# T4's split behind the second pair's evictions, the third pair's products reordered, and C22's transposes placed in mid-slice

## The chip, the core and the metric

One Trainium2 chip (trn2), one NeuronCore of it. The metric is the device time of one execution in microseconds (us), as the median of several runs. TensorE multiplies, VectorE and ScalarE read its accumulators, GpSimd works between buffers, and SyncE issues most of the transfers.

## What is computed

A decoder block on 1024 positions of width 1024: a short gated convolution and a forgetting attention side by side, merged by gates, and then a gated feed-forward with a causal convolution of three taps. The change lies in the last part, the feed-forward, cut here to what matters:

```
h2 = rmsnorm(x, norm2_g) * (1 + sc2) + sh2
u = h2 @ w_up                       # (1024, 2 * 2816)
u = causal_dwconv(u, conv_ffn_w)    # three taps over positions
gate, val = split(u, 2)
ff = (silu(gate) * val) @ w_down    # (1024, 1024)
x = x + g2 * ff
```

All is float32. The kernel makes each product from three: it splits both operands into a high part (H, rounded to the matmul's input type) and a low part (L, the rest), and sums H x H, H x L and L x H in an accumulator.

## The kernel before

**The up projection.** It runs over 22 slices f of 128 gate and 128 value columns, each with one accumulator g (gate) and one v (value) of 128 x 1024, two banks each; four such accumulators exist. The first three slices, u0, u1 and u2 (called pairs here, of gate and value weights), use plain products: `plain(n, half)` multiplies one half of the weights' rows (n // 2) of gate or value (n % 2) with a block of h2 for one half of the positions. A product is twelve matmuls of 512 columns. The blocks are B11 and B21 (first half of positions) and B12 and B22 (second half).

The other 19 slices use Strassen's scheme in Winograd's form, with seven products p1 to p7 in place of eight, from B11, B21, B22 and the combinations T1 to T4 of blocks. Block B12 and combination T4 share one buffer (L1553), so T4 may be written only when u2's products from B12 are done; it is read by each slice's last product, p4.

**The order around the first slice.** From L1459 on the order on TensorE, VectorE, ScalarE and GpSimd is the order of the program text; SyncE's is chosen by the scheduler. L1765 to L1787 make T1 to T3 with u0's evictions in between. L1790 to L1792 are u2's eight products. Then follow T4's four high parts (ScalarE, `split_h`, L1446) and low parts (VectorE, `split_l`, L1452). Behind them stand u1's evictions: `scale_g` and `scale_v` (ScalarE, L1676), `taps_g` and `taps_v` (VectorE, L1680, two each), `silu` (ScalarE, L1702), `ff` (VectorE, L1705) and its store. Between them stands `U[3].x_split()`, which splits the first Strassen slice's weights x (wh on ScalarE, L93, wl on VectorE, L94). Then come that slice's sums of weights on GpSimd (L1593, L1594, L1599) and their splits (L1559, L1560). In the loop from L1809, p1 reads x, `snap` copies p1's bank to s1 (ScalarE, L1633), p7 writes the other bank of the same accumulator, and `u2` adds s1 into U2 (VectorE, L1625).

The buffers tagged u, eight of 128 x 1024, hold x1 (the block's input blocks, from which T1 to T4 are made) and later the evicted gate and value.

**The down projection.** Again seven products, in the order `ORDER = (1, 5, 6, 3, 7, 2, 4)`, each over eleven steps c of twelve matmuls into four banks e. In each step the operands of the step after next are split (ScalarE L1918, VectorE L1919). The four banks of a finished product are added to the output tiles xo in the next product's steps, one bank at a time (`x_add`, VectorE, L1950). A tile that is complete is turned in the step behind: four 128 x 128 transposes on TensorE into the bank just added (`x_turn_out`, L1961), a copy to ot (ScalarE, L1967) and the store (SyncE). Product 3 completes one tile for each e. Product 2 completes two, (0, 0) and (1, 1), which is C22, and both are turned in the same bank, one behind the other, in four steps of the last product (p = 4). Banks e = 0 and 1, and banks e = 2 and 3, are the two halves of one accumulator there.

Of the kernel before, what the change touches and what calls it, by code (L numbers as in the profile page):

```python
# [33 lines left out]
def tile_hybrid_block(  # L34
# [110 lines left out]
    NK = ND // 2  # L145
# [308 lines left out]
    class Token:  # L454
# [5 lines left out]
        def copy(self):  # L460
            q = f32(self.keep[:, 0]) if self.keep else bp.tile([P, 512], F32, tag="qn", name="q", bufs=6)
            scalar.activation(q, self.src, AF.Copy)
            self.src, self.copied = q, True
# [57 lines left out]
    def tok_mm(j, acc, cuts, units, t0):  # L521

        outs = [acc[:, 512 * i : 512 * i + c1 - c0] for i, (c0, c1) in enumerate(cuts)]
        for dd in range(ND):
            for f in events.pop(t0 + dd, ()):
                f()
            w = units[dd // 2]
            for t in TERMS:
                for o, (c0, c1) in zip(outs, cuts):
                    mm(o, h_slice(t[0], dd, j), w[t[1]][:, dd % 2, c0:c1],  # L530
                       start=dd == 0 and t == TERMS[0], stop=dd == ND - 1 and t == TERMS[2])
        return outs
# [142 lines left out]
    for i in range(8):  # L675
        t = T1K + TSK * i
# [220 lines left out]
    for n, j in enumerate((4, 5, 6, 7, 0, 1, 2, 3)):  # L897
# [7 lines left out]
        t = Token(j, tok_mm(j, acc, FULL, qunits, t0)[0], q_d, qg)  # L905
# [293 lines left out]
    steps = [(h, ip) for h in range(NH) for ip in range(4)]  # L1199
# [91 lines left out]
    def acc4(nm):  # L1291
        return psD.tile([P, S], F32, tag="acc", name=nm, bufs=4)
# [419 lines left out]
    def blocks(kk):  # L1712
        return x1[kk][:, lo], x1[kk][:, hi], x1[kk + NK][:, lo], x1[kk + NK][:, hi]
# [14 lines left out]
    def t_op(kk, n, low):  # L1728

        b11, b12, b21, b22 = blocks(kk)  # L1730
        dst, src, shift = ((T3, b12, db[:, kk : kk + 1]), (T2, b22, None), (T1, b11, None), (T4, b21, None))[n]
        (split_l if low else split_h)(dst, kk, src, shift)
# [4 lines left out]
    u0, u1, u2 = U[:N0]  # L1737
# [49 lines left out]
            U[3].fetch(up)  # L1787
    u2.xs = wsp[4:6]
    u2.g, u2.v = (acc4(nm) for nm in ("upg", "upv"))
    for n in (0, 2, 1, 3):  # L1790
        for half in range(2):
            u2.plain(n, half)  # L1792
    for kk in range(NK):
        t_op(kk, 3, False)
        t_op(kk, 3, True)
    u1.scale_g()
    u1.scale_v()
    u1.taps_g()
    u1.silu()
    U[3].x_split()  # L1800
    u1.taps_v()
    u1.ff()
    u1.ff_out()
# [64 lines left out]
    def ff_load(f, half):  # L1868
        sync.dma_start(ff[f][:, half], ff_d[f][:, half])
# [68 lines left out]
    steps = [Step(p, c) for p in ORDER for c in range(NC)]  # L1938

    def banks_for():  # L1940
        ts = [acc4("dn") for _ in range(2)]
        return [t[:, sl] for t in ts for sl in (lo, hi)]

    def x_add(p, e, bank, b0=0, nb=4):

        ij = ADDS[p]
        bl = slice(b0 * P, (b0 + nb) * P)
        t = xo[e, *ij][:, bl]
        g = g2[:, e + 4 * ij[0] : e + 4 * ij[0] + 1]
        vector.scalar_tensor_tensor(out=t, in0=bank[:, bl], scalar=g, in1=t, op0=ALU.mult, op1=ALU.add)  # L1950
        turns.extend((e, ij, bank) for ij in STORE.get(p, ()))

    def x1_load(e, i, j):
        sync.dma_start(xo[e, i, j], x1_d[e + 4 * i][:, hsl[j]])

    def x_turn_out(e, ij, bank, b0=0, nb=4, copy=None):

        i, j = ij
        bl = slice(b0 * P, (b0 + nb) * P)
        for n in range(b0, b0 + nb):  # L1960
            tensor.transpose(bank[:, n * P : (n + 1) * P],  # L1961
                             xo[e, i, j][:, n * P : (n + 1) * P], ident)
        ot = gp2.tile([P, 512], F32, tag="ot", name="ot", bufs=3)
        if copy:
            copy(ot[:, bl], bank[:, bl])
        else:
            scalar.activation(ot[:, bl], bank[:, bl], AF.Copy)  # L1967
        d0, t0 = (e + 4 * i) * P, 512 * j + b0 * P
        sync.dma_start(out[0, t0 : t0 + nb * P, d0 : d0 + P].rearrange("(j p) d -> p j d", p=P),
                       ot[:, bl].rearrange("p (j d) -> p j d", j=nb))  # L1970
# [18 lines left out]
    adds, turns = [], []  # L1989
    NE = 3  # L1990
    for t, st in enumerate(steps[: len(steps) - NE + 1]):
        n = t // NC
        if st.c == 0 and t:
            if n == 1:
                sets.append(banks_for())
            done, old = steps[t - 1].p, sets[(n + 1) % 2]
            adds = [lambda p=done, e=e, b=old[e]: x_add(p, e, b) for e in range(4)]
        banks = sets[n % 2]
        if t == T0:
            upS.close()  # L2000
            gp2 = ctx.enter_context(tc.tile_pool(name="ff2", bufs=1, side="left", reuse_waits="tile"))
            skeep += [gp2.tile([P, 512], F32, name=f"s{c}") for c in range(NC)]
            xo = {(e, i, j): gp2.tile([P, 512], F32, name=f"xo{e}{i}{j}") for e in range(4) for i, j in ((0, 0), (1, 1), (0, 1))}
            xo |= {(e, 1, 0): xo[e, 0, 1] for e in range(4)}
        for _ in range(2 if t < 26 else 1):
            if ff_loads:
                ff_load(*ff_loads.pop(0))
        for k in range(4 if t == 0 else t + AHEAD, min(t + AHEAD + 1, len(steps))):
            steps[k].load()
        for k in range(3 if t == 0 else t + 3, min(t + 4, len(steps))):  # L2010
            steps[k].sums()
        if st.p in X1 and T0 <= st.c < T0 + 4:
            x1_load(st.c - T0, *X1[st.p])
        if t + 2 < len(steps):
            steps[t + 2].split()
        for w in ends.get(t, ()):
            w()
        while turns:
            x_turn_out(*turns.pop(0))
        if st.c > 0 and adds and (st.c % 2 == 0 or st.p == ORDER[-1]):  # L2020
            adds.pop(0)()
        if t < len(steps) - NE:
            st.mm(banks)
    last = steps[-NE:]

    def finish(e):
# [47 lines left out]
```

## Time and profile before

| | us |
|---|---|
| median of three runs | 1474.64 |
| lowest and highest | 1472.72, 1478.87 |
| the profiled execution | 1473.5 |
| its span, first to last instruction | 1471.5 |

The profile's page gives for each engine its busy time, the share of the span and the number of instructions. Views of the trace give the same for stretches of time, list instructions of an engine in order of time with the idle time in front of each and what ended it, and name the wait that ended last. Times in the trace count from the span's start.

### The profile page before, as it was taken

To read this page: it belongs to the slowest core of one execution; us is meant where nothing else is said; L and a number is where in the kernel's file an instruction comes from. 1 tells how busy PE (TensorE), PEld (TensorE's weight loads), DVE (VectorE), ACT (ScalarE), POOL (GpSimd) and SP (SyncE) were. 2 spreads that over 40 slices of the span, in tenths; PEclk is the share of its full clock that TensorE was granted. 3 is DMA by queue.
4 is the path that set the end of the run, shared out by engine and by line. 5 is a ranking of instruction groups with operands and counts; after the bars stand their busy time and mean duration, and the time that the engine had idled before them with its cause. 6 is when DMAs were issued, how large, how long until landed. Compare 5 with 4: busy or idle time off the path is not lost. (4 is left out here: it accounts for less than half of the span.)

```text
span 1471.5 us, 19375 instructions
## 1 busy us (share of the span) xinstructions
PE 1403.4 (95%) x6668; PEld 1155.1 (78%) x6668; DVE 1099.4 (75%) x1828; ACT 651.8 (44%) x1104; POOL 504.1 (34%) x532
## 2 busy tenths in 40 slices
PE   5889889999999999899999999999999999999997
PEld 4679668887888888778788877888888887888876
DVE  7965798888777776456846858777777776898764
ACT  6554453434455454555414534333333333444443
POOL 3646666665555553323221013333333331000000
PEclk9999999999999999999999999999999999999999
DMA  9539654437664557776962122222222213983722
GB/s 286 160 105 322 199 163 129 132 95 209 159 169 115 146 133 227 225 244 219 244 164 83 44 72 86 86 87 86 86 86 86 72 36 116 390 311 103 213 80 77
DMA packets 260759, 222.44 MB, mean 151 GB/s; under 512 B 43117, under 2 KB 213445, under 8 KB 260661
## 3 DMA queue, kind: packets, MB, share of 16 engines
q1 hardware_dynamic: 259389, 218.61, 49.6%
q0 software_dynamic: 1136, 2.56, 0.6%
q8 instruction: 52, 0.85, 0.2%
q14 instruction: 46, 0.38, 0.1%
q10 hardware_dynamic: 136, 0.04, 0.0%
HBM read 169.76 MB, written 51.41 MB: 150 GB/s over the span
## 5 line engine op out<-in xcount | busy, mean ns | idle before, releaser
L1925 PE MATMUL dn<-bL,aH 128*128 128x512 f32 x308 | 120.5, 391 | 0.6 <-DVE bL L1919 0.6
L1925 PE MATMUL dn<-bH,aH 128*128 128x512 f32 x308 | 120.8, 392 | 0.0
L1925 PE MATMUL dn<-bH,aL 128*128 128x512 f32 x308 | 120.0, 390 | 0.0
L1559 ACT ACTIVATE wh<-ws 128x512 fp32r<-128x512 f32 x95 | 55.5, 627 | 133.8 <-POOL ws L1593 131.0
L730 DVE TENSOR_TENSOR ol<-ws,oh 128x512 fp32r<-128x512 f32 x98 | 94.6, 974 | 14.1 <-ACT oh L729 11.6
L94 DVE TENSOR_TENSOR wl<-ws,wh 128x1024 fp32r<-128x1024 f32 (+1 forms) x51 | 70.0, 1373 | 40.6 <-ACT wh L93 40.1
L729 ACT ACTIVATE oh<-ws 128x512 fp32r<-128x512 f32 x98 | 61.2, 626 | 70.9 <-PE pacc L775 38.6
L1593 POOL TENSOR_TENSOR ws<-ws 128x512 f32<-128x512 f32 x19 | 24.7, 1300 | 187.7 <-DVE wl L94 187.7
L1162 ACT ACTIVATE L<-L,mn 128x256 f32<-128x256 f32 (+6 forms) x56 | 46.4, 829 | 60.7 <-DVE mn L1160 58.9
L1165 POOL TENSOR_SCALAR L<-L,rs 128x384 f32<-128x384 f32 (+7 forms) x62 | 48.3, 779 | 69.8 <-DVE rs L1164 68.6
L1925 PEld LDWEIGHTS dn<-bL,aH 128*128 128x128 f32 x308 | 57.8, 188 | 14.1 <-DVE bL L1919 2.7
L1185 ACT ACTIVATE th<-pt 128x512 fp32r<-128x512 f32 (+1 forms) x80 | 43.5, 551 | 55.3 <-PE pt L1179 53.7
L559 POOL TENSOR_TENSOR ws<-ws 128x512 f32<-128x512 f32 x42 | 55.1, 1312 | 36.5 <-DVE ol L730 17.1
L1925 PEld LDWEIGHTS dn<-bH,aH 128*128 128x128 f32 x308 | 57.8, 188 | 12.3 <-ACT bH L1918 0.4
L1925 PEld LDWEIGHTS dn<-bH,aL 128*128 128x128 f32 x308 | 57.8, 188 | 11.9
L93 ACT ACTIVATE wh<-ws 128x1024 fp32r<-128x1024 f32 (+1 forms) x58 | 60.8, 1052 | 12.3 <-DMA ws<-in_w_branch_a_dram 4.1
L1560 DVE TENSOR_TENSOR wl<-ws,wh 128x512 fp32r<-128x512 f32 x76 | 64.2, 864 | 2.3 <-ACT wh L1559 2.3
L1918 ACT ACTIVATE aH<-dws 128x512 fp32r<-128x512 f32 x52 | 32.8, 631 | 74.6 <-issue 41.0
L1680 DVE SCALAR_TENSOR_TENSOR u<-upv,cwT,u 128x1023 f32<-128x1023 f32 (+1 forms) x44 | 56.4, 1282 | 10.7 <-ACT u L1676 9.9
L1186 DVE TENSOR_TENSOR tl<-pt,th 128x512 fp32r<-128x512 f32 (+1 forms) x80 | 50.3, 634 | 18.5 <-ACT th L1185 17.1
L439 POOL TENSOR_TENSOR wacc<-wacc,wa 128x256 f32<-128x256 f32 x48 | 43.5, 907 | 55.8 <-ACT wa L438 52.4
L1919 DVE TENSOR_TENSOR aL<-dws,aH 128x512 fp32r<-128x512 f32 x52 | 35.9, 690 | 34.2 <-ACT aH L1918 34.2
(561 smaller groups left out, 4503.0 us busy)
## 6 DMA issues: line engine op xcount, KB each, us to landing
wa<-in_w_ada_dram SPq DMA_DIRECT2D x48, 512.0 KB
dws<-in_w_down_dram SPq DMA_DIRECT2D x96, 256.0 KB
ws<-in_w_up_dram SPq DMA_DIRECT2D x44, 512.0 KB
ws<-in_w_in_dram SPq DMA_DIRECT2D x36, 512.0 KB
ff<-ff_d SPq DMA_DIRECT2D x44, 256.0 KB
ff_d<-u SPq DMA_DIRECT2D x21, 512.0 KB
xt<-in_x_dram SPq DMA_DIRECT2D x8, 512.0 KB
v_d<-vt SPq DMA_DIRECT2D x8, 512.0 KB
```

Of the source, the lines that this page charges most:

```text
L93: scalar.activation(wh[:, : n * m], ws[:, : n * m], AF.Copy)
L94: eng.tensor_tensor(out=wl[:, : n * m], in0=ws[:, : n * m], in1=f32(wh[:, : n * m]), op=ALU.subtract)
L559: gpsimd.tensor_tensor(out=o, in0=a, in1=b, op=ALU.subtract)
L729: scalar.activation(h, src, AF.Copy)
L730: eng.tensor_tensor(out=l, in0=src, in1=f32(h), op=ALU.subtract)
L1162: scalar.activation(L[:, :n], L[:, :n], AF.Exp, scale=-1.0, bias=mn, accum_out=sm)
L1165: eng.tensor_scalar(out=L[:, :n], in0=L[:, :n], scalar1=rs, scalar2=0.0, op0=ALU.mult, op1=ALU.add)
L1186: vector.tensor_tensor(out=flat[2][:, c0:], in0=flat[0][:, c0:], in1=f32(flat[1][:, c0:]), op=ALU.subtract)
L1559: scalar.activation(ops[0][:, sl], src, AF.Copy)
L1560: eng.tensor_tensor(out=ops[1][:, sl], in0=src, in1=f32(ops[0][:, sl]), op=ALU.subtract)
L1680: vector.scalar_tensor_tensor(out=u[:, s:], in0=acc[:, : S - s], scalar=cwT[:, 2 - s, n : n + 1], in1=u[:, s:], op0=ALU.mult, op1=ALU.add)
L1925: mm(banks[e], self.A[i][:, es_], self.B[j], start=self.p in FIRST and self.c == 0 and t == 0, stop=self.c == NC - 1 and t == 2, skip_grou ...
```

## The change

It has two places. In the up projection u2's eight products come in another order, with the two from B12 first; and T4's splits move from ahead of u1's `scale_g` to behind `U[3].x_split()`. In the down projection the first tile turned in a step stays ahead of the step's products; a second one is turned after the products of the first two banks, and the step's `x_add` now stands between the two.

```diff
@@ -1787,17 +1787,16 @@
     u2.g, u2.v = (acc4(nm) for nm in ("upg", "upv"))
-    for n in (0, 2, 1, 3):
-        for half in range(2):
-            u2.plain(n, half)
-    for kk in range(NK):
-        t_op(kk, 3, False)
-        t_op(kk, 3, True)
+    for n, half in ((0, 1), (1, 1), (0, 0), (2, 0), (2, 1), (1, 0), (3, 0), (3, 1)):
+        u2.plain(n, half)
     u1.scale_g()
     u1.scale_v()
     u1.taps_g()
     u1.silu()
     U[3].x_split()
+    for kk in range(NK):
+        t_op(kk, 3, False)
+        t_op(kk, 3, True)
     u1.taps_v()
     u1.ff()
     u1.ff_out()
@@ -2015,12 +2014,18 @@
-        while turns:
-            x_turn_out(*turns.pop(0))
+        first, second = turns[:1], turns[1:]
+        turns.clear()
+        for a in first:
+            x_turn_out(*a)
         if st.c > 0 and adds and (st.c % 2 == 0 or st.p == ORDER[-1]):
             adds.pop(0)()
-        if t < len(steps) - NE:
-            st.mm(banks)
+        st_es = (range(2), range(2, 4)) if second else (range(4),)
+        for n, es in enumerate(st_es):
+            if n:
+                x_turn_out(*second[0])
+            if t < len(steps) - NE:
+                st.mm(banks, es)
```

## Rows read from the trace of the kernel before

**Rows 1.** The page: engine, busy us (share of the span) xinstructions.

```profile
PE 1403.4 (95%) x6668; PEld 1155.1 (78%) x6668; DVE 1099.4 (75%) x1828; ACT 651.8 (44%) x1104; POOL 504.1 (34%) x532
```

**Rows 2.** Stretches: length, busy (x) PE, PEld, DVE, ACT, POOL, clock, DMA share, GB/s.

```profile
856.94:859.74 2.80, 2.80 (x14) 2.27 (x12) 0.00 (x0) 0.00 (x0) 0.00 (x0) 1.00 0.00 0
867.90:893.13 25.23, 21.33 (x86) 15.43 (x85) 20.64 (x21) 9.98 (x14) 10.34 (x8) 1.00 0.33 105
893.13:912.54 19.41, 19.41 (x85) 15.79 (x84) 15.40 (x17) 8.18 (x12) 7.34 (x6) 1.00 0.26 82
912.54:931.88 19.34, 19.34 (x85) 15.79 (x84) 15.06 (x17) 7.28 (x10) 6.45 (x6) 1.00 0.26 81
```

**Rows 3.** Timeline of TensorE, first slice: start, length, instruction, [idle before, releaser].

```profile
869.16 0.50 PE L1569 MATMUL upv<-B11H,wh 128*128 128x512 f32 x1 [0.87 <-ACT wh L93]
...
870.42 0.50 PE L1569 MATMUL upv<-B11H,wl 128*128 128x512 f32 x1 [0.53 <-DVE wl L94]
...
877.37 0.50 PE L1569 MATMUL upv<-T3H,wh 128*128 128x512 f32 x1 [1.34 <-ACT s L1633]
...
884.23 0.50 PE L1569 MATMUL upv<-T1H,wl 128*128 128x512 f32 x1 [0.56 <-DVE wl L1560]
...
887.39 0.47 PE L1569 MATMUL upg<-B22H,wh 128*128 128x512 f32 x1 [0.59 <-DVE U L1625]
```

**Rows 4.** Timeline of ScalarE ahead of the first slice.

```profile
860.64 2.73 ACT L1446 ACTIVATE T4H<-x 128x512 fp32r<-128x512 f32 x4 [19.14 <-PE upv L1569]
863.27 1.10 ACT L1676 ACTIVATE u<-upg,cwT 128x1024 f32<-128x1024 f32 x1
...
867.11 1.06 ACT L1702 ACTIVATE u<-u 128x1024 f32<-128x1024 f32 x1 [1.73 <-DVE u L1680]
868.07 1.04 ACT L93 ACTIVATE wh<-ws 128x1024 fp32r<-128x1024 f32 x1
```

**Rows 5.** Timeline of VectorE ahead of the first slice.

```profile
843.13 2.59 DVE L1680 SCALAR_TENSOR_TENSOR u<-upv,cwT,u 128x1023 f32<-128x1023 f32 x2
845.65 1.22 DVE L94 TENSOR_TENSOR wl<-ws,wh 128x1024 fp32r<-128x1024 f32 x1
...
861.30 2.79 DVE L1452 TENSOR_TENSOR T4L<-x,T4H 128x512 fp32r<-128x512 f32 x4 [11.44 <-ACT T4H L1446]
...
869.14 1.23 DVE L94 TENSOR_TENSOR wl<-ws,wh 128x1024 fp32r<-128x1024 f32 x1 [2.13 <-ACT wh L93]
870.28 2.60 DVE L1680 SCALAR_TENSOR_TENSOR u<-upv,cwT,u 128x1023 f32<-128x1023 f32 x2
```

**Rows 6.** Timeline of GpSimd, its first work in this part.

```profile
870.45 1.30 POOL L1593 TENSOR_TENSOR ws<-ws 128x512 f32<-128x512 f32 x1 [72.38 <-DVE wl L94]
```

**Rows 7.** Stretches of the down projection: one turn, two turns four times, none.

```profile
1371.33:1374.56 3.23, 3.23 (x18) 2.73 (x17) 3.23 (x6) 1.64 (x3) 0.00 (x0) 1.00 0.70 225
1430.58:1450.26 19.68, 15.38 (x81) 12.34 (x81) 10.25 (x16) 8.96 (x17) 0.00 (x0) 1.00 0.38 107
1450.26:1452.98 2.72, 2.72 (x13) 2.25 (x12) 1.90 (x3) 1.15 (x3) 0.00 (x0) 1.00 0.00 1
```

**Rows 8.** Timeline of TensorE, transposes of the steps with two turns.

```profile
1430.58 0.64 PE L1961 MATMUL dn<-ident,xo 128*128 128x128 f32 x4
1432.29 0.66 PE L1961 MATMUL dn<-ident,xo 128*128 128x128 f32 x4 [1.08 <-ACT ot L1967]
...
...
1447.03 0.66 PE L1961 MATMUL dn<-ident,xo 128*128 128x128 f32 x4 [1.05 <-ACT ot L1967]
```

**Rows 9.** Timeline of ScalarE, first copy of the first of these steps.

```profile
1431.65 0.58 ACT L1967 ACTIVATE ot<-dn 128x512 f32<-128x512 f32 x1
```

**Rows 10.** Timeline of VectorE in two of these steps.

```profile
1431.87 0.68 DVE L1919 TENSOR_TENSOR bL<-ff,bH 128x512 fp32r<-128x512 f32 x1
1433.61 0.75 DVE L1950 SCALAR_TENSOR_TENSOR xo<-dn,mod,xo 128x512 f32<-128x512 f32 x1 [1.06 <-ACT ot L1967]
...
1437.43 0.74 DVE L1950 SCALAR_TENSOR_TENSOR xo<-dn,mod,xo 128x512 f32<-128x512 f32 x1
```

## The prediction

> **What bounds the kernel now.** I read the page first: TensorE is busy 95% of the span, and no other engine over 75% [rows 1]. So a microsecond is won only where TensorE stands still, and only if nothing else is late at the same place. I then looked for its idle time after 780 us by a table of stretches and by its own timeline. In the loop over 19 feed-forward slices a slice takes 19.3 to 19.4 us with TensorE busy throughout, but the first one, counted from the last product of the third pair (u2), takes 25.23 [rows 2]. Five waits stand in it [rows 3]: two for the split of its weights x (wh, then wl), one for the copy s1 (snap), one for wl of the next weights, one for the U2 sum. The second place is the last phase (p = 4): the four steps that turn output tiles take 19.68 us together, against 2.72 for a step without turns and 3.23 for a step of an earlier phase with one turn [rows 7]. In each of the four the second turn's transposes wait about 1.1 us for ScalarE's copy of the first (1.08 in the first step, 1.05 in the fourth) [rows 8]. The granted clock is 1.00 in all these stretches [rows 2, 7], so no term for the clock enters.
>
> **Why the first slice is late.** ScalarE stands idle for 19.14 us, until 860.64, because its next four instructions write T4 over B12 and wait for u2's products from B12; VectorE idles 11.44 us behind it [rows 4, 5]. Queued behind on the same two engines are u1's evictions (scale, taps, silu) and the split of the first slice's weights, whose wh ends at 869.11 and wl at 870.37 [rows 4, 5]. TensorE had finished u2 at 868.13 (last start 867.90 plus 0.23). GpSimd's sums for the same slice wait for that wl, after 72.38 us of idleness [rows 6].
>
> **Part 1, order of u2's products.** The eight products are the same, 2.80 us each [rows 2]; nothing is added. They start at 845.74 (four of them before 856.94). Those from B12 become first and second, so B12 is free at 845.74 + 5.60 = 851.3 instead of 862.5. The price is cover: the first product into u2.v moves from 856.94 to 848.54. Its accumulators are those of u0.v, whose last tap ends at 845.72, and its weights are split by 846.87 [rows 5]. That leaves 2.8 and 1.7 us; below that each microsecond would be lost once. I cost it at nothing. u2.g is complete one product later, 859.74, far ahead of its eviction.
>
> **Part 2, T4 behind u1's evictions.** ScalarE is free at 841.50 (860.64 less 19.14) and VectorE at 849.86 (861.30 less 11.44) [rows 4, 5]. With durations of these rows, and buffers u taken as free only when VectorE's last T split ends: scale_g 849.9 to 851.0, taps_g (2.60) to 853.6, silu (1.06) to 854.7, x wh (1.04) to 855.7, x wl (1.23) to 857.0. Then T4's high parts on ScalarE to 858.4 (2.73; B12 is free since 851.3) and low parts on VectorE to 859.8 (2.79), taps_v to 862.4, and ff behind it. GpSimd's two sums run 857.0 to 859.6, the queue being empty. What moves with ff is SyncE's store of ff and what is queued behind it there; both go earlier by 10 us, as taps_v does (870.28 before), and no transfer is added.
>
> Against TensorE's needs: p1 at 868.13 needs x wl, ready 11 us before. p2 at 870.9 needs u1.v's accumulators (taps_v), 8.5 us before. p7 at 873.7 needs snap, which runs as p1 ends, the split ahead of it on ScalarE being done by about 867; some 2 us of cover. p5 at 879.3 needs its wl, which follows snap, scale_v (1.1) and taps_v (2.6), about 876. T4 itself is read at 884.8. So all five waits go, and the slice becomes one like the next: 25.23 less 0.23 (the ordinary step) less 19.41 = **5.6 us**. Bounds: if only the waits for wh and wl go, 869.16 less 868.13, and 0.53 plus some 0.2 of restart, 1.8; at most 5.7, by the 19.34 us slice. I take 5.6, since the later waits are all for engines that have run late since 860. After that TensorE runs without a gap to the down projection, and every later event hangs on it, so the shift is carried to the end.
>
> **Part 3, the second turn in mid-slice.** Per step the same eight transposes and twelve products, no new transfer. One turn costs 3.23 less 2.72 = 0.51, so a step with two and no wait takes 3.74. Call a step's start 0. The first turn and six products last to about 1.87 (0.51 and 6 x 0.227). The first copy ends at 1.65 (1431.65 + 0.58 less 1430.58) [rows 8, 9], so it just hides, with 0.2 to spare.
>
> But the change puts an x_add between the two turns, and it reads a bank of the same two-bank accumulator in two of the four steps: tile e = 1 in the step that turns e = 0, and e = 3 with e = 2. The trace shows that waits hold for the whole accumulator: p7 writes the left half of upv and waited for snap, which reads the right half [rows 3]; the x_add of e = 1 waited until 1433.6 for the second copy of e = 0, while that of e = 2, on another accumulator, ran at 1437.43 right behind its predecessor [rows 10]. So the second transposes would wait for that x_add: it issues 0.6 behind bL (1431.87), at 1.9, lasts 0.75, ends at 2.65, and transposes start at 2.7 where they could at 1.87. That is 0.8 twice. Sum of the four: 3.74 x 4 + 2 x 0.8 = 16.6 against 19.68, a gain of **3.1 us**. Without the new wait it is 19.68 less 14.96 = 4.7, the upper bound. The lower is 0, where the second transposes start as late in the step as each saving is worth (below).
>
> By the Trainium skill, "PSUM — Partial Sum Buffer", section "PSUM bank collisions raise a hardware error", engines have to be kept apart only by bank and quadrant of partitions, and a different bank is free; by that rule the x_add would hold nothing up and the gain would be 4.7. The two waits above stand against it: what the program waits for is coarser here.
>
> **Sum.** 5.6 + 3.1 = 8.7 us off the profiled execution's 1473.5: 1464.8. The median of the runs shown is 1474.6, 1.1 above the profiled one, so 1465.9.
>
> **Rivals.**
> 1. *The bank rule holds, no new wait in mid-slice.* 5.6 + 4.7 = 10.3: 1464.3. For it: the two banks differ. Against it: rows 3 and 10. Chance 0.17.
> 2. *Another wait follows in the first slice.* Snap or the U2 sum stays late, because T4's four splits now stand ahead of u1's second taps and ff on VectorE; only the two waits for x go: 1.8 + 3.1 = 4.9, 1469.7. For it: VectorE is busy 20.6 of 25.2 us there [rows 2]. Against it: it starts 11 us earlier. Chance 0.16.
> 3. *Slower than before: the pace of the products.* In the trace a product takes 2.72 us in the last phase (one step) and 2.80 in u2 with no wait named [rows 2, 7]; a slice of 19.37 is a mixture, seven at 2.80 would be 19.60. If the order of writes to buffers sets the pace, and all after u2 went at 2.80, it would cost 19 x 0.23 = 4.4 in the slices and 77 x 0.08 = 6.1 in the down projection, 10.5: 1476.4. It decides once over 83% (8.7 of 10.5) of those products are slow. Against it: operands, buffers and order in the loop stay as they were. Chance 0.05.
> 4. *The change in mid-slice does nothing* (the second transposes start at 3.0 or later in each step, as x_add or copy comes 0.4 to 1.2 late): 5.6 alone, 1469.0. Chance 0.10.
>
> My forecast has 0.52.
>
> **How the numbers follow.** About 0.5%, 7.4 us, is what a measurement of this kernel can tell from no change; the bound is 1467.3. The forecast lies 1.4 under it and the three times shown before spread by 6, so of its 0.52 I give 0.43 to faster and 0.09 to same. Rival 1 is faster; rivals 2 and 4 are same, but for 0.05 by scatter; rival 3 is half same, half slower. With that, faster 0.65, same 0.32, slower 0.03. The range of 8 in 10 reaches from rival 1 less 1.5 of scatter to rival 2 plus 1: 1462.5 to 1470.7.
>
> **What would show each step.** ScalarE must go from u1's scales to x's split before T4, with T4 starting near 855.7 without a wait for products. The step from u2's last product to p1 is 0.23; the stretch to the second slice's p1 lasts 19.6 to 19.7. VectorE's x_add of e = 1 and e = 3 starts 1.9 into its step; the second transposes start at 2.7 there and at 1.9 in the other two steps, which take 4.6 and 3.7 us. I'm wrong if p7 or p3 of the first slice still waits over 0.5 us, if u2's second product waits for u0.v, or if slices after the first are longer than 19.4.

## The result, and the profile after

The median fell from 1475.16 us (four runs, 1472.72 to 1478.87) to 1465.70 (four runs, 1463.42 to 1467.13): ratio 0.9932, 95% interval 0.9907 to 0.9958. That is a gain of 6.2 to 13.7 us. The forecast was 1465.9. The profiled execution of the changed kernel took 1466.52 us, its span 1464.8, against 1473.5 and 1471.5.

Two profiles are best compared by stretches that begin and end at the same instruction, since the work ahead of the change varies: u2's first product started at 845.74 us in the profile of before and at 847.86 in this one, though nothing ahead of it differs (in all twelve profiles of this document it starts between 839.1 and 850.4, a wider spread than the change is worth). First before, then after: u2's first product to the second slice's p1; the four steps with two turns; from there to the span's end. Columns as in [rows 2].

```profile
845.74:893.13 47.39, 43.49 (x181) 33.28 (x180) 30.09 (x32) 15.31 (x20) 10.34 (x8) 1.00 0.28 89
...
1450.26:1471.55 21.29, 16.18 (x77) 12.72 (x75) 8.04 (x13) 5.50 (x10) 0.00 (x0) 0.98 0.18 50
```

```profile
847.86:889.45 41.59, 41.59 (x181) 33.84 (x180) 31.73 (x32) 15.99 (x21) 11.87 (x9) 1.00 0.33 102
1426.60:1443.02 16.42, 15.10 (x81) 12.06 (x81) 10.08 (x16) 8.98 (x17) 0.00 (x0) 1.00 0.40 113
1443.02:1464.82 21.80, 16.22 (x77) 12.72 (x75) 8.04 (x13) 5.50 (x10) 0.00 (x0) 0.95 0.22 61
```

The first stretch lost 5.80 us and TensorE is busy in all of it. The four steps lost 3.26 (19.68 in [rows 7]). The end grew by 0.5, which is no part of the change (below). Between the first and the second stretch lie 537.45 us before and 537.15 after. In the ten other profiles below it is 536.9 to 538.2, so no effect of the change shows there. Together 5.80 + 3.26 + 0.30 - 0.51 less the late start of 2.12 is the 6.73 by which the two spans differ.

The slice after the first is as before (19.41 and 19.34 in [rows 2]):

```profile
889.45:908.85 19.40, 19.40 (x86) 15.80 (x85) 15.00 (x17) 7.37 (x11) 6.53 (x6) 1.00 0.26 82
908.85:928.18 19.33, 19.33 (x85) 15.79 (x84) 15.07 (x17) 7.28 (x10) 6.44 (x6) 1.00 0.27 81
```

ScalarE ahead of the first slice, timeline of after, the rows that answer to [rows 4]:

```profile
850.23 1.12 ACT L1676 ACTIVATE u<-upg,cwT 128x1024 f32<-128x1024 f32 x1 [6.60 <-DVE u L1705]
...
854.59 1.06 ACT L1702 ACTIVATE u<-u 128x1024 f32<-128x1024 f32 x1 [2.00 <-DVE u L1680]
855.55 1.04 ACT L93 ACTIVATE wh<-ws 128x1024 fp32r<-128x1024 f32 x1
856.50 2.18 ACT L1446 ACTIVATE T4H<-x 128x512 fp32r<-128x512 f32 x4
...
873.04 0.60 ACT L1633 ACTIVATE s<-upv 128x512 f32<-128x512 f32 x1 [4.17 <-PE upv L1569]
```

The 19.14 us of waiting for products from B12 are gone. u1's `scale_g` now waits 6.60 us for VectorE's `ff` of u0 (that `ff` frees the buffer u which it takes is read from this releaser, and not tested); T4's splits find B12 free; snap waits only for its own product. VectorE and GpSimd beside it, which answer to [rows 5] and [rows 6]:

```profile
856.63 1.22 DVE L94 TENSOR_TENSOR wl<-ws,wh 128x1024 fp32r<-128x1024 f32 x1 [2.13 <-ACT wh L93]
857.77 4.69 DVE L1452 TENSOR_TENSOR T4L<-x,T4H 128x512 fp32r<-128x512 f32 x4
862.38 2.59 DVE L1680 SCALAR_TENSOR_TENSOR u<-upv,cwT,u 128x1023 f32<-128x1023 f32 x2
```

```profile
857.93 1.69 POOL L1593 TENSOR_TENSOR ws<-ws 128x512 f32<-128x512 f32 x1 [57.75 <-DVE wl L94]
859.70 1.62 POOL L1594 TENSOR_TENSOR ws<-ws 128x512 f32<-128x512 f32 x1
```

x is split by 857.85, where p1 starts at 870.10. In the down projection TensorE's transposes, which answer to [rows 8], and VectorE's `x_add`, to [rows 10]:

```profile
1426.60 0.63 PE L1960 MATMUL dn<-ident,xo 128*128 128x128 f32 x4
1429.30 0.65 PE L1960 MATMUL dn<-ident,xo 128*128 128x128 f32 x4 [0.67 <-DVE xo L1949]
1431.18 0.60 PE L1960 MATMUL dn<-ident,xo 128*128 128x128 f32 x4
1433.02 0.60 PE L1960 MATMUL dn<-ident,xo 128*128 128x128 f32 x4
1434.85 0.60 PE L1960 MATMUL dn<-ident,xo 128*128 128x128 f32 x4
1437.48 0.66 PE L1960 MATMUL dn<-ident,xo 128*128 128x128 f32 x4 [0.64 <-DVE xo L1949]
```

```profile
1428.50 0.75 DVE L1949 SCALAR_TENSOR_TENSOR xo<-dn,mod,xo 128x512 f32<-128x512 f32 x1
```

The four waits for the copy are gone, and two for `x_add` stand in their place, in the first and the third step: 4.58 us (1426.60 to 1431.18) and 4.52, where the other two take 3.67 and 3.65.

### The profile page after: what moved, and what is told of

The parts are those of the page before. It is cut to its first block, busy times and chain, and to the rows that moved or that the text cites. A ratio compares the mean times of both kernels' runs of the same rounds, so it can differ in the third digit from the quotient of the medians.

```text
span 1464.8 us, 19377 instructions
## 1 busy us (share of the span) xinstructions
PE 1405.2 (96%) x6668; PEld 1159.3 (79%) x6668; DVE 1101.4 (75%) x1828; ACT 651.4 (44%) x1104; POOL 503.7 (34%) x532
## 5 line engine op out<-in xcount | busy, mean ns | idle before, releaser
L1560 POOL TENSOR_TENSOR wl<-ws,wh 128x512 fp32r<-128x512 f32 x19 | 24.7, 1299 | 107.3 <-ACT wh L1559 107.3
```

What stands on the lines that cost most here:

```text
L1560: eng.tensor_tensor(out=ops[1][:, sl], in0=src, in1=f32(ops[0][:, sl]), op=ALU.subtract)
```

## The experiments

Measured by the same three stretches in the profile of each kernel (us). e3 to e7 ran once each and are read by these stretches alone; their whole times were 1469.46, 1464.79, 1460.61, 1463.16 and 1468.67 us. The other whole times follow with each.

| kernel | u2 to second slice | four steps | from there to the end |
|---|---|---|---|
| before | 47.39 | 19.68 | 21.29 |
| changed | 41.59 | 16.42 | 21.80 |
| e1_up_only | 41.59 | 19.74 | 21.28 |
| e2_down_only | 47.39 | 16.42 | 21.93 |
| e3_move_only | 41.74 | 16.42 | 22.30 |
| e4_order_only | 41.59 | 16.41 | 22.65 |
| e5_other_banks | 41.59 | 14.65 | 21.29 |
| e6_add_behind | 41.59 | 15.31 | 21.35 |
| e7_v_first | 42.38 | 16.43 | 21.33 |
| e8_banks_ot4 | 41.59 | 14.64 | 21.31 |
| e9_after_again | 41.60 | 16.42 | 21.34 |
| e10_banks_again | 41.59 | 14.65 | 22.65 |

**Each part alone.** Do the two gains add, and does anything give them back? e1_up_only keeps the up projection's part (against the changed kernel; the rest of the step goes back likewise):

```diff
-        first, second = turns[:1], turns[1:]
...
+        while turns:
+            x_turn_out(*turns.pop(0))
...
```

> The up projection's part alone (u2's order and T4's place), the down projection as before. Theory: the two parts add. From u2's first product to the second slice's p1: 47.4 us before, 41.6 here, as in the changed kernel; the four steps with two turns keep 19.7 us. Time 5.6 to 5.8 below the kernel before, ratio 0.996. Rival: part of the early gain is given back later and shows only together with the other part; then the ratio stays within 0.999.

e2_down_only keeps the other:

```diff
-    for n, half in ((0, 1), (1, 1), (0, 0), (2, 0), (2, 1), (1, 0), (3, 0), (3, 1)):
-        u2.plain(n, half)
+    for n in (0, 2, 1, 3):
+        for half in range(2):
+            u2.plain(n, half)
+    for kk in range(NK):
+        t_op(kk, 3, False)
+        t_op(kk, 3, True)
     u1.scale_g()
...
-    for kk in range(NK):
-        t_op(kk, 3, False)
-        t_op(kk, 3, True)
     u1.taps_v()
```

> The down projection's part alone. Theory: the stretch in the up projection stays 47.4 us; the four steps take 16.4 us in place of 19.7, with two waits of about 0.65 for VectorE's x_add and none for the copy. Time 3.1 to 3.3 lower, ratio 0.998. Rival: the final chain (last splits, last stores) takes the gain back, ratio 1.000 and a longer stretch behind the four steps.

Ratio 0.9960 (0.9944 to 0.9977) for the first, 0.9968 (0.9954 to 0.9982) for the second; their product, 0.9928, is the ratio of both together within its interval. By the medians the kernels are 6.35 and 3.33 us below the kernel before, where 5.6 to 5.8 and 3.1 to 3.3 were expected. Each shows its own stretch shortened and the other as before. The gains are separate. Only the end was longer in e2's profile (21.93), to which the last experiments come.

**Which edit of the first part does it.** e3_move_only has u2's products in the order of before, T4 in its new place:

```diff
-    for n, half in ((0, 1), (1, 1), (0, 0), (2, 0), (2, 1), (1, 0), (3, 0), (3, 1)):
-        u2.plain(n, half)
+    for n in (0, 2, 1, 3):
+        for half in range(2):
+            u2.plain(n, half)
```

> T4's splits behind u1's evictions and x's split, but u2's products in the order of before, so that B12 is free six products after u2's start (16.8 us) in place of two (5.6). Theory: x's split is early (no wait at p1), but T4, and behind it on ScalarE and VectorE the next weights' splits, snap and u1's second taps are late: p7 waits about 1.5 for snap and p5 about 0.5; from u2's first product to the second slice's p1 43.5 to 44.5 us (41.6 in the changed kernel, 47.4 before). Rival: the place of T4 alone does it, 41.6.

e4_order_only has the new order, T4 in its old place:

```diff
         u2.plain(n, half)
+    for kk in range(NK):
+        t_op(kk, 3, False)
+        t_op(kk, 3, True)
     u1.scale_g()
...
     U[3].x_split()
-    for kk in range(NK):
-        t_op(kk, 3, False)
-        t_op(kk, 3, True)
```

> u2's products in the new order, T4's splits in their old place ahead of u1's evictions. Theory: B12 is free 5.6 us after u2's start, T4's splits take ScalarE and VectorE until about 9.3 us, x's split ends about 15.7 us after u2's start, 6 to 7 us before p1 needs it: no wait in the first slice, 41.6 us from u2's first product to the second slice's p1. So the order alone would give the whole gain. Rival: both edits are needed, over 43 us.

Both take all five waits out: 41.74 and 41.59 us. The 0.15 between them lies in u2's eight products, which last 22.39 us in the old order (before, e3) and 22.24 in the new (e4, the changed kernel); why the order changes their pace stays open. For e4 the 41.6 was expected. ScalarE in e4, T4's splits and x's split:

```profile
847.93 2.73 ACT L1446 ACTIVATE T4H<-x 128x512 fp32r<-128x512 f32 x4 [7.92 <-PE upv L1569]
...
855.36 1.04 ACT L93 ACTIVATE wh<-ws 128x1024 fp32r<-128x1024 f32 x1
```

There x is split by 857.67, 8.8 us before p1 starts at 866.47. For e3 I was wrong and the rival right: the place of T4 alone does it too. ScalarE in e3:

```profile
865.25 2.73 ACT L1446 ACTIVATE T4H<-x 128x512 fp32r<-128x512 f32 x4 [6.15 <-PE upv L1569]
...
874.47 0.63 ACT L1559 ACTIVATE wh<-ws 128x512 fp32r<-128x512 f32 x1 [4.97 <-POOL ws L1599]
875.68 0.60 ACT L1633 ACTIVATE s<-upv 128x512 f32<-128x512 f32 x1 [0.58 <-PE upv L1569]
```

T4 still waits 6.15 us, and begins 14.9 us after u2's first product (850.35), not 16.8: its first quarter needs only the first quarter of B12, not both products from B12 whole. That was to be seen in the trace of before, where T4 began at 860.64 [rows 4] and those products ended at 862.5; in e4 it began 3.7 us after u2's first product (844.23), where I had expected 5.6. The next weights' split (874.47) ends before snap can start, and p7, which starts at 878.21, has its cover of about 2 us. The 1.9 us don't account for all of my miss: with them added to these rows snap would end at about 877.6 (an estimate), still ahead of p7, so that the 1.5 us of waiting for it were too much in any case. What else was wrong in that forecast stays open. So order and place each suffice to take the waits out, which cost 5.65 us; the other 0.15 of the 5.80 goes with the order alone.

**The cover in u2.** e7_v_first exchanges u2's first two products:

```diff
-    for n, half in ((0, 1), (1, 1), (0, 0), (2, 0), (2, 1), (1, 0), (3, 0), (3, 1)):
+    for n, half in ((1, 1), (0, 1), (0, 0), (2, 0), (2, 1), (1, 0), (3, 0), (3, 1)):
```

> The changed kernel with u2's first two products exchanged, so that the product into u2.v, on u0.v's accumulators and with the weights split last, is the first. Theory: the cover that I counted (2.8 us for the accumulators, 1.7 for wl) is real: without it the third matmul waits about 0.7 us for wl, and the stretch from u2's first product to the second slice's p1 is 42.2 to 42.5 us in place of 41.6. Rival: both are ready anyway, 41.6.

42.38, as expected, by one wait (timeline of TensorE, e7):

```profile
850.56 0.50 PE L1569 MATMUL upv<-T4H,wl 128*128 128x512 f32 x1 [0.55 <-DVE wl L94]
```

The weights' low part is what the second place in the order covers. The accumulators of u0.v showed no wait even so: their last tap ended at 849.37 us, and the first product into them started at 849.38.

**What the second transposes wait for.** e5_other_banks deals out the second set of banks so that tiles e and e + 1 lie in different accumulators:

```diff
-                sets.append(banks_for())
+                b = banks_for()
+                sets.append([b[e] for e in (0, 2, 1, 3)])
...
-    pt = [old[e] for e in (0, 2, 1, 3)]
+    pt = old
```

> The changed kernel with the second set of accumulator banks dealt out as the first is, so that tiles e and e + 1 lie in different accumulators. Theory: the waits of the second transposes for VectorE's x_add (0.67 and 0.64 in the changed kernel) are there only because x_add reads the other bank of the same accumulator; without that all four steps take 3.67 us, together 14.7 in place of 16.4. Rival: x_add's place between the turns is what counts, whichever accumulator it reads; then 16.4 stays.

e6_add_behind keeps the banks and puts `x_add` behind the second turn:

```diff
-        if st.c > 0 and adds and (st.c % 2 == 0 or st.p == ORDER[-1]):
-            adds.pop(0)()
         st_es = (range(2), range(2, 4)) if second else (range(4),)
...
                 st.mm(banks, es)
+            if n == len(st_es) - 1 and st.c > 0 and adds and (st.c % 2 == 0 or st.p == ORDER[-1]):
+                adds.pop(0)()
```

> The changed kernel with its own banks, but x_add put behind the second turn. Theory: the second transposes wait no more, but x_add waits for the second copy (about 3.1 us into the step), ends at 3.9, and the next step's first transposes wait 0.2 to 0.3 for it in two of the four steps: 15.1 to 15.4 us. Rival: no wait for the copy of another bank, 14.7.

Transposes of e5's first two steps and its `x_add` beside the second of them, then `x_add` and the transposes behind it in e6:

```profile
1422.69 0.64 PE L1960 MATMUL dn<-ident,xo 128*128 128x128 f32 x4
1424.55 0.60 PE L1960 MATMUL dn<-ident,xo 128*128 128x128 f32 x4
1426.38 0.60 PE L1960 MATMUL dn<-ident,xo 128*128 128x128 f32 x4
1428.20 0.60 PE L1960 MATMUL dn<-ident,xo 128*128 128x128 f32 x4
```

```profile
1424.59 0.74 DVE L1949 SCALAR_TENSOR_TENSOR xo<-dn,mod,xo 128x512 f32<-128x512 f32 x1
```

```profile
1427.86 0.75 DVE L1949 SCALAR_TENSOR_TENSOR xo<-dn,mod,xo 128x512 f32<-128x512 f32 x1 [1.14 <-ACT ot L1966]
```

```profile
1428.66 0.66 PE L1960 MATMUL dn<-ident,xo 128*128 128x128 f32 x4
```

In e5 `x_add` still stands between the turns and runs while the second transposes do, and no transpose waits: 14.65 us, all four steps alike. In e6 `x_add` waits 1.14 us for ScalarE's copy from the other bank of its accumulator, and the next step's first transposes come 0.24 late (1428.66 less 1426.59 is 2.07, against 1.83 in e5): 15.31. So the wait belongs to the accumulator as a whole, and moving `x_add` only changes who waits.

**A version that takes the wait out.** e8_banks_ot4 is e5 with a fourth buffer ot, after the last copy of the changed kernel had waited for a store (the last row of ScalarE's timeline, after):

```profile
1460.87 0.38 ACT L1966 ACTIVATE ot<-dn 128x256 f32<-128x256 f32 x1 [1.44 <-DMA out_dram<-ot]
```

```diff
-        ot = gp2.tile([P, 512], F32, tag="ot", name="ot", bufs=3)
+        ot = gp2.tile([P, 512], F32, tag="ot", name="ot", bufs=4)
```

> The other banks and a fourth buffer ot. In the changed kernel the last copy waits 1.44 us for the store of a buffer used three copies before, since one of that store's 16 parts lands late beside a 16 KB instruction transfer. Theory: with a fourth buffer the last copy waits for TensorE alone; from the end of the four steps to the end of the span 21.0 to 21.4 us (21.8 in the changed kernel, 21.3 before), the four steps 14.7. Sum 2.0 to 2.3 us below the changed kernel, about 11 below the kernel before, ratio 0.9925. Rival: the last store lands as late as before and the end stays at 21.8 or more.

e9_after_again is the changed kernel and e10_banks_again is e8, side by side on one chip.

> The changed kernel itself, beside the next one on one chip. Ratio to the kernel before 0.993 to 0.995. From the last transposes to the end of the span 4.9 us if no 16 KB instruction transfer falls on the last stores, 5.4 to 6.2 if one does; that it did in the profile of the changed kernel would then be chance and not the change.

> The version with the other banks and four buffers ot again, timed beside the changed kernel. Theory: 1.8 us less in the four steps and nothing given back, so its median lies 1.5 to 2.5 us below that of the changed kernel in the same rounds. Rival: the end takes it back, medians within 0.5 us.

e8: median 1465.80, ratio 0.9946 (0.9934 to 0.9958). e9: 1466.23, 0.9944 (0.9928 to 0.9961). e10: 1463.25, 0.9926 (0.9911 to 0.9941). The four steps are 1.8 us shorter in both profiles, so the version does what it should there. By whole times the forecasts missed. e8 is 8.0 us below the kernel before, not about 11, and the forecast ratio of 0.9925 lies outside its interval; e10 is 3.0 below the changed kernel in the same rounds, where 1.5 to 2.5 was forecast. e8's ratio even lies above that of the changed kernel's first measurement (0.9932): the runs don't tell 1.8 us apart.

The fourth buffer's worth stays open. e8's end took 21.31 us, but those of e5, e7 and e9 took 21.29 to 21.34 with three buffers, and e10's took 22.65 with four. The stretch to the end goes by something else. In the seven profiles with 21.28 to 21.35 us, no 16 KB instruction transfer (queue q8) starts between 3 us before the last transpose and the end; the nearest ones ahead, 3.8 us before it in e8 and 4.4 in e6, cost nothing. In the five with 21.80 to 22.65, the changed kernel, e2, e3, e4 and e10, one does. The granted clock of the stretch doesn't sort them: 0.92 in e8, 0.97 in e10. The DMA view of the last 8 us, e9 and then after, in 40 slices:

```profile
DMA  0000299999999700000199999999800000000100
GB/s 0 0 0 0 85 298 242 329 296 281 288 288 291 224 13 0 0 0 0 57 301 265 311 275 281 301 278 291 252 23 0 0 0 0 0 0 0 41 0 0
```

```profile
DMA  0019999999981000019999306979920000000100
GB/s 0 0 36 273 324 291 291 266 273 276 286 235 41 20 23 20 23 56 299 289 289 286 108 0 202 273 202 281 278 72 0 0 0 0 0 0 0 41 0 0
...
q8 instruction: 1, 0.02, 0.7%
```

In the changed kernel the first stores trail off at 20 to 23 GB/s for about a microsecond; in e9, the same kernel without the transfer, they end sharply, and the end takes 21.34 us. The trace has 16 landings for each store. In the first two of the changed kernel fifteen come within 0.25 us and the last one 1.30 and 1.09 us behind them. All five profiles with such a transfer have one to three stores whose last landing is 1.0 to 1.5 us late; in the seven others none is over 0.07. In the changed kernel and e2 these are the first two stores, and the last copy waits for one of them, a wait that a fourth buffer should take out, though no run shows it; in e4 and e10 they are the last three, which no copy waits for.

## Why the prediction was right

- **What bounds the kernel.** It held: both gains were idle time of TensorE, and no other engine became the bound behind them. The sum was 8.7 us; the stretches show 5.80 + 3.26 = 9.06, and the median of before less that of after is 9.5. That the median came within 0.2 us of the forecast is in part luck: the gain was 0.8 larger than forecast, and the median before rose by 0.5 with the fourth run. The profiled execution was forecast at 1464.8 and took 1466.52, mainly because u2 started 2.12 us later than before. By its own sum the range should start at 1462.8 (1464.3 less 1.5), not at 1462.5; the result lies inside either.
- **Part 1, the order at no cost.** Right, and the cover is real: e7 took it away and paid 0.79 us, for the low part of the weights, which I had given 1.7 us of cover. The 2.8 us for the accumulators were right too: with all of it used in e7, the first product started as the last tap ended, without a wait.
- **Part 2, 5.6 us.** Measured 5.80, above the 5.7 that I had called the most. Of the 0.2 over 5.6, about 0.15 lies in u2's products, whose pace I had taken as unchanged: the stretch from u2's first product to p1 fell from 23.42 to 22.24 us, 1.18, where the wait for wh was 1.03. The order of events held, and all came early: with u2's start moved from 845.74 to 847.86, `scale_g` was forecast at 852.0 and started at 850.23, x wl was to end at 859.1 and did at 857.85, T4 to begin at 857.8 and did at 856.50. I had u's buffers free too late: `scale_g` started when u0's `ff` ended. T4's low parts, forecast at 2.79 us, took 4.69 beside GpSimd's sums, a cost that I had put at nothing and that stayed under cover. What I missed is that either edit alone would do (e3, e4).
- **Part 3, 3.1 us.** Measured 3.26. The new wait was forecast at 0.8 twice and showed as 0.67 and 0.64 of idle time, 0.91 and 0.85 from step to step (4.58 and 4.52 less 3.67, with the restart). The two steps without it were forecast at 3.74 and took 3.67 and 3.65.
- **Rival 1, banks apart by the rule of the Trainium skill** ("PSUM — Partial Sum Buffer", "PSUM bank collisions raise a hardware error"). The page states what the chip needs; what this program waits for is the whole accumulator, and e5 and e6 show it: the measurement decides, and for this kernel the rule's 14.96 us came true only when the tiles were dealt to different accumulators (14.65).
- **Rivals 2, 3 and 4.** No wait was left in the first slice (41.59 us, all busy). The pace of the products stayed: 19.40 and 19.33 us a slice, and from the down projection's first product to the turns 188.8 us before and 188.6 after. The copy hid: 1427.68 plus 0.58 is 1428.26, and six products end at about 1428.46.

## What to carry to other kernels

When an engine that works in order waits at the head of its queue, read what stands behind it: here T4's split, first read 17 us after the start of p1, held up the split that p1 itself needs, and either moving it back or freeing its buffer earlier was enough. Before work is put between two steps to hide a wait, list what else is issued there and which accumulator it touches, whole tiles rather than banks; the neighbour that shares one becomes the next wait. Compare profiles between like instructions: here the same instruction started up to 11 us apart in profiles with the same code ahead of it, and the end varied by 1.4 us.

## What the runs showed of the hardware

T4's four low parts took 4.69 us on VectorE in the changed kernel and 2.79 in e3, where GpSimd's sums were over before they began (2.79 also in before and e4, where the sums came later); beside them GpSimd's two sums took 1.69 and 1.62 us against 1.29 there. Rows of e3, VectorE and GpSimd:

```profile
865.91 2.79 DVE L1452 TENSOR_TENSOR T4L<-x,T4H 128x512 fp32r<-128x512 f32 x4 [5.56 <-ACT T4H L1446]
```

```profile
860.43 1.29 POOL L1593 TENSOR_TENSOR ws<-ws 128x512 f32<-128x512 f32 x1 [57.76 <-DVE wl L94]
861.79 1.29 POOL L1594 TENSOR_TENSOR ws<-ws 128x512 f32<-128x512 f32 x1
```

The Trainium skill, "SBUF — State Buffer", section "Who interferes with whom", says that a VectorE instruction with two inputs in that memory contends with one of GpSimd that reads it. The rows agree, and here both sides paid: 1.9 us on VectorE and 0.7 on GpSimd, all of it under cover.

Where an instruction transfer of 16 KB fell on the last stores, the end of the kernel was 0.5 to 1.4 us longer (21.80 to 22.65 against 21.3), with the same code once with it (the changed kernel's profile) and once without (e9), and one of the 16 landings of a store came 1.0 to 1.5 us behind the others. That the transfer is the cause is read from these twelve profiles, and no run set it on purpose.
